# SBUF offsets of the matmul operands: stationary tiles at multiples of 64 bytes, moving weights 32 bytes off

## The chip, the cores and the metric

The kernel runs on one core of a Trainium2 chip. The metric is the device time of one launch in microseconds: the kernel before has a median of 1641.32 us over three runs (1641.16 to 1642.12). TensorE multiplies, VectorE (DVE), ScalarE (ACT) and GpSimd (POOL) do the rest, and the DMA queue of SyncE (SP) brings the weights in.

## The reference, cut to what matters

One transformer-like block on 256 tokens of width 2048, all in float32: a token mixer (spatial gating beside gated linear attention), a cross attention over a memory of 256 rows, and a feed-forward layer with a short convolution. Nearly all of its arithmetic is in products of an activation with a weight matrix:

```
z = h @ w_in                       # h 256x2048, w_in 2048x12304, cut into sg, q, k, v, og, ma, mb
merged = sigmoid(m_a) * (y_a @ w_proj_a) + sigmoid(m_b) * (y_b @ w_proj_b)
y = merged @ w_out
...                                # cross attention: xa_wq, xa_wk, xa_wv, xa_wo
hid = h @ w_up                     # 2048 x 11264
y = (gelu(gate) * up) @ w_down     # 5632 x 2048
```

## The kernel before, in words

**Split products.** A product in float32 is made of three in the type float32r: each operand x is split into `hi`, its rounding, and `lo` = x - `hi`, and the products hi*hi, hi*lo and lo*hi are summed in PSUM. A weight unit of 128 x 2048 comes in by one DMA (`load_raw`, three buffers `raw`), is split half by half by `split_half` (ACT rounds into `hi`, line 89; DVE subtracts into `lo`, line 90; four buffers of each, from the pool `wpool`), and is used at once. Activations are split once per stage by `split_psum`, and live in tiles of shape [128, k, 2, 256], hi beside lo: `hT`, `yaT`, `ybT`, `mT`, `fT`, `h2T` (also called `hT` in the code), `oT`, `act`.

**Two kinds of product.** A matmul has a stationary operand, brought into the array by a load (LDWEIGHTS, shown as PEld), and a moving one that streams past it.

- `tok_mm` (lines 106 to 108) is used in the stages sg, v, og, m, p, mix, xv, xa and ffn. The *activation* is stationary (128 columns), and 512 columns of `hi` or `lo` *weights* move. Three matmuls of 512 moving columns make one step.
- `feat_piece` (lines 137, 138, 140 and 141) is used in the stages k, q, xk, xq and up. The *weights* are stationary, and the activation moves: 512 columns against `hi` (its hi and lo halves together), 256 columns against `lo`. A pair of such matmuls makes one step. The stage up has 88 blocks of 16 pairs, k and q eight blocks each, xk and xq four each.

Line 449 writes out the first sg product, line 637 is the product `o` of the gated attention (moving `v`, stationary `AS`).

**What sets the order.** A scheduler orders the instructions from a model of times, except in the parts under `manual_schedule`. The pools place tiles one behind the other in SBUF, in the order in which they are opened, so a tile's address follows from the sizes of those before it. `const` and `stat` are small pools whose tiles begin at multiples of 32 bytes.

Of the kernel before, what the change touches and what calls it, by code (L numbers as in the profile page):

```python
# [11 lines left out]
F32 = mybir.dt.float32  # L12
F32R = mybir.dt.float32r
# [4 lines left out]
P = 128  # L18
# [3 lines left out]
KD = D // P  # L22
# [10 lines left out]
EPS = 1e-6  # L33
UW = 2048
HW = 1024

C_MIX, C_XA, C_MEM, C_FFN = 0, KD, 2 * KD, 3 * KD
C_CB = 4 * KD
# [6 lines left out]
def block_kernel(ctx: ExitStack, tc: tile.TileContext, a, out):  # L45
    nc = tc.nc

    def pool(stack, name, bufs=1, space=None, side=None):
        kw = {"space": space} if space is not None else {}
        if side is not None:  # L50
            kw["side"] = side
        return stack.enter_context(tc.tile_pool(name=name, bufs=bufs, **kw))

    const = pool(ctx, "const")
    wpool = pool(ctx, "wpool")
# [23 lines left out]
        while later:  # L79
            step()  # L80

    def split_half(raw, p=None, into=None, eng=None):
        p = wpool if p is None else p
        if into is None:
            hi = p.tile([P, HW], F32R, tag="hi", bufs=4, name="hi")
            lo = p.tile([P, HW], F32R, tag="lo", bufs=4, name="lo")
        else:
            hi, lo = into
        nc.scalar.copy(out=hi, in_=raw)  # L89
        (eng or nc.vector).tensor_tensor(out=lo, in0=raw, in1=hi.bitcast(F32), op=ALU.subtract)  # L90
        return hi, lo

    def load_raw(src):
        raw = wpool.tile([P, UW], F32, tag="raw", bufs=3, name="raw")
        nc.sync.dma_start(out=raw, in_=src)
        return [raw[:, i * HW:(i + 1) * HW] for i in range(UW // HW)]

    def pieces(w, n, nu):
        for u in range(nu):
            for half in load_raw(w[n, u]):  # L100
                yield split_half(half)

    def tok_mm(ps, xT, k, t, wh, wl, first, last):
        xh = xT[:, k, 0, t * P:(t + 1) * P]
# [5 lines left out]
    def tok_piece(ps, xT, i, t, hi, lo, K, nw=512):  # L110
        kp = HW // nw
        for kk in range(kp):
# [16 lines left out]

    def feat_piece(ps, xT, i, hi, lo, kks=range(HW // P)):  # L130
        for kk in kks:
# [10 lines left out]

    def feat_block(w, j, xT, name, srcs=None):
        ps = mm_psum(f"{name}_{j}")
        for i, (hi, lo) in enumerate(srcs if srcs is not None else pieces(w, j, KD * P // UW)):
            feat_piece(ps, xT, i, hi, lo)
            step()
        return ps
# [165 lines left out]
    mt = ctx.enter_context(ExitStack())  # L314
    with ExitStack() as mix:
        mp = pool(mix, "mp", side="left")
        hT = mp.tile([P, KD, NT, S], F32R, name="hT")
        yaT = mp.tile([P, SGW // P, NT, S], F32R, name="yaT")
        gl = mix.enter_context(ExitStack())
# [16 lines left out]
        with ExitStack() as st2:  # L336
# [67 lines left out]
            with tc.manual_schedule():  # L404
                nc.scalar.dma_start(out=gmix, in_=a["cols"][:, C_MIX:C_MIX + KD])
                first.append(wpool.tile([P, 2, 2, 512], F32, tag="raw", bufs=3, name="raw"))
                for k in (0, 1):
                    for n in range(2):
                        nc.sync.dma_start(out=first[0][:, n, k, :], in_=a["w_sgv"][0, :, n, k, :])
                        if n == 0:  # L410
                            load_xt(k, 1)
                load_xt(2, 2, nc.scalar)
                load_unit([(slice(0, 2), k) for k in range(2)])
                load_xt(4, 2)
                load_unit()
                warm_up(10)
                pss = [[mm_psum(f"sg_{n}_{t}") for t in range(NT)] for n in (2, 3)]
                for i in range(KD // 2):
                    if 1 <= i < KD // 2 - 2:
                        if i % 2:  # L420
                            load_xt(2 * i + 4, min(4, KD - 2 * i - 4))
                        load_unit()
                    hl = []
                    for n in range(2):
                        hi = wpool.tile([P, HW], F32R, tag="hi", bufs=4, name="hi")
                        lo = wpool.tile([P, HW], F32R, tag="lo", bufs=4, name="lo")
                        hl.append((hi, lo))
                    if i < 2:
                        for k in range(2):
                            c = slice(k * 512, (k + 1) * 512)  # L430
                            for n, (hi, lo) in enumerate(hl):
                                split_half(first[i][:, n, k, :], into=(hi[:, c], lo[:, c]))
                                if n == 0:
                                    gain_x(2 * i + k)
                    else:
                        gain_x(2 * i)
                        gain_x(2 * i + 1)
                        for n, x in enumerate(hl):
                            split_half(first[i][:, n, :, :].rearrange("p k c -> p (k c)"), into=x)
                    square_x(i)  # L440
                    later_loads(i)
                    for k in (2 * i, 2 * i + 1):
                        if k == KD - 1:
                            token_rstd()
                        c = slice(k % 2 * 512, (k % 2 + 1) * 512)
                        for n, (hi, lo) in enumerate(hl):
                            for j, (part, w) in enumerate(((0, hi), (1, hi), (0, lo))):
                                for t in range(NT):
                                    nc.tensor.matmul(pss[n][t], hT[:, k, part, t * P:(t + 1) * P], w[:, c],  # L449
                                                     start=k == 0 and j == 0, stop=k == KD - 1 and j == 2)  # L450
                ps = mm_psum("glr")
                for k in range(KD):
                    nc.tensor.matmul(ps[0:80, :], wg[:, k, :, :], hT[:, k, :, :], start=k == 0, stop=k == KD - 1)

                row_bcast(rs, rbc, "mix")
# [189 lines left out]

        mpool = pool(mt, "mtp", side="right")
        mT = mpool.tile([P, KD, NT, S], F32R, name="mT")
        with ExitStack() as st:
            sp = pool(st, "mg", side="right")
            for n in range(4):  # L650
                acc = [None] * NT
                for wm, wp, yT, K in ((a["w_ma"], a["w_pa"], yaT, SGW // P), (a["w_mb"], a["w_pb"], ybT, KD)):
                    ps = tok_block(wm, n, hT, KD, "m")
                    sgs = []
                    for t in range(NT):
                        sg = sp.tile([P, 512], F32, tag="sgm", bufs=3, name=f"sgm_{n}_{t}")
                        nc.scalar.activation(out=sg, in_=ps[t], func=AF.Sigmoid, scale=rs[t])
                        sgs.append(sg)
                    ps = tok_block(wp, n, yT, K, "p")
                    for t in range(NT):  # L660
                        pr = sp.tile([P, 512], F32, tag="pr", bufs=5, name=f"pr_{n}_{t}")
                        nc.vector.tensor_tensor(out=pr, in0=ps[t], in1=sgs[t], op=ALU.mult)
                        if acc[t] is None:
                            acc[t] = pr
                        else:
                            nc.vector.tensor_tensor(out=pr, in0=pr, in1=acc[t], op=ALU.add)
                            later.append(partial(transp_split, pr, t, mT, 4 * n, f"mt_{n}_{t}"))
            flush()
# [11 lines left out]
    with ExitStack() as xa:  # L680
# [106 lines left out]
        with tc.manual_schedule():  # L787
# [26 lines left out]
                        tok_piece(pss[n, t], oT, i, t, *early[2 * n + i], H)  # L814
            ups = [load_raw(a["w_up"][j, 0]) for j in (0, KF)]
            ups = [[raw[i] for raw in ups] for i in range(2)]
            ups[0] = [split_half(raw, eng=eng) for raw, eng in zip(ups[0], (nc.vector, nc.gpsimd))]
            for n in (0, 1):
                for t in range(NT):
                    pn.leave(pss[n, t], n, t, gain_first=t == 1)  # L820
# [52 lines left out]
            for q in range(4):  # L873
                gain_out2(tps[2 * q:2 * q + 2], C_FFN, fT, 2 * q)
                if q < 2:
                    pn.add(1, q + 2)
                    ups[1][q] = split_half(ups[1][q])
                if q == 3:
                    up1 = [split_half(half) for half in load_raw(a["w_up"][1, 0])]
                square3(1, q)  # L880
                for ps, (hi, lo) in zip(up_ps, ups[q // 2]):
                    feat_piece(ps, fT, q // 2, hi, lo, range(q % 2 * 4, q % 2 * 4 + 4))
                if q < 2:
                    up_in(q + 2)
# [7 lines left out]
    with ExitStack() as ff:  # L892
        fp = pool(ff, "ff", side="right")
        act = fp.tile([P, KF, NT, S], F32R, name="act")
        with ExitStack() as up:
            tp_ = pool(up, "tp_", side="left")
            rb3 = tp_.tile([P, S], F32, name="rb3")
# [128 lines left out]
```

## Time and profile before

| | us |
|---|---|
| median of three runs | 1641.32 |
| the profiled execution | 1642.16 |
| its span, first to last instruction | 1640.5 |
| TensorE busy with matmuls | 1628.3 |
| weight loads | 1372.4 |
| DVE busy | 1044.1 |
| ACT busy | 845.9 |

A matmul's busy time in the profile runs on past the start of the next one: matmuls are pipelined. Of use is the spacing from one start to the next. It is read either from rows of the timeline, or from a window full of matmuls, as its length over the number of matmuls in it. That number counts those that lie across the window's ends too. Where a matmul shows 0.39 us and the spacing is 0.227 us, some 1.7 are in flight at any time, and so many are counted too often.

### The profile page before, as it was taken

The page shows a single profiled execution, that of the slowest core. Times are in us where ns is not written, and L with a number is a line of the kernel's source. Part 1 is how long each engine was busy: PE and PEld are TensorE (multiplying, and loading weights), DVE is VectorE, ACT ScalarE, POOL GpSimd, SP SyncE. Part 2 cuts the span into 40 slices and gives each one's busy share as a digit, 9 for nine tenths or more (in the row PEclk, how much of TensorE's full clock was granted, in tenths as well). Part 3 has the DMA queues.
Part 4 walks back from the last instruction along what each step waited for, and adds up shares of the span by engine and source line. Part 5 has one row for each costly group of instructions (what it writes and reads, how often), then busy time and mean ns, then how long its engine had stood idle before and what let it go on. Part 6 is the DMA issues. An engine that isn't in the chain of part 4 may idle for free.

```text
span 1640.5 us, 20820 instructions
## 1 busy us (share of the span) xinstructions
PE 1628.3 (99%) x8090; PEld 1372.4 (84%) x8090; DVE 1044.1 (64%) x1398; ACT 845.9 (52%) x1174; POOL 40.0 (2%) x127
## 2 busy tenths in 40 slices
PE   9999999999999999999999999999999999999997
PEld 7888888888888888888888888888888888888886
DVE  7777645555454545465766877777777777444444
ACT  7764444444444444464656655555555555344342
POOL 0100000000000000000002000000000000000000
PEclk9999999999999999999999999999999999999999
DMA  9554455555555555595553555555545555555553
GB/s 330 180 196 168 172 200 179 178 178 180 186 192 191 190 195 183 204 356 196 189 206 103 189 191 186 182 184 199 181 180 191 191 183 206 205 181 198 187 199 107
DMA packets 47699, 315.43 MB, mean 192 GB/s; under 512 B 5392, under 2 KB 6032, under 8 KB 10864
## 3 DMA queue, kind: packets, MB, share of 16 engines
q1 hardware_dynamic: 47312, 313.83, 53.5%
q8 instruction: 63, 1.03, 0.2%
q14 instruction: 36, 0.29, 0.1%
q10 hardware_dynamic: 288, 0.27, 0.0%
HBM read 311.98 MB, written 2.10 MB: 191 GB/s over the span
## 4 chain that ended last, share of the span: by engine, by line
PE 96%; ACT 1%; DVE 1%; DMA 1%; issue 1%; SPq 0%; DVEq 0%; POOLq 0%; POOL 0%; ACTq 0%
PE up L137 19%; PE up L138 10%; PE ffn L106 5%; PE ffn L108 5%; PE ffn L107 5%; PE m L107 4%; PE m L106 4%; PE m L108 4%; PE p L107 3%; PE p L106 3%; PE p L108 3%; PE sg L449 2%; PE mix L108 2%; PE mix L107 2%; PE v L107 2%; PE v L108 2%
## 5 line engine op out<-in xcount | busy, mean ns | idle before, releaser
L90 DVE TENSOR_TENSOR lo<-raw,hi 128x1024 fp32r<-128x1024 f32 (+1 forms) x567 | 689.2, 1218 | 444.6 <-ACT hi L89 436.1
L89 ACT CAST hi<-raw 128x1024 fp32r<-128x1024 f32 (+1 forms) x568 | 591.5, 1044 | 524.5 <-PE ffn L107 129.6
L137 PE MATMUL up<-fT,hi 128*128 128x512 f32 x1320 | 470.4, 399 | 0.4 <-DVE fT L210 0.4
L138 PE MATMUL up<-fT,lo 128*128 128x256 f32 x1320 | 370.7, 281 | 0.0
L137 PEld LDWEIGHTS up<-fT,hi 128*128 128x128 f32 x1320 | 248.0, 188 | 57.6 <-DVE fT L210 0.7
L138 PEld LDWEIGHTS up<-fT,lo 128*128 128x128 f32 x1320 | 249.3, 189 | 4.2
L106 PE MATMUL ffn<-hi,act 128*128 128x512 f32 x352 | 138.7, 394 | 0.0
L108 PE MATMUL ffn<-lo,act 128*128 128x512 f32 x352 | 137.7, 392 | 0.0
L107 PE MATMUL ffn<-hi,act 128*128 128x512 f32 x352 | 136.6, 388 | 0.0
L903 ACT COPY hd<-up 128x256 f32<-128x256 f32 x88 | 32.8, 374 | 139.7 <-PE up L141 139.7
L106 PE MATMUL m<-hi,hT 128*128 128x512 f32 x256 | 100.0, 391 | 0.0
L108 PE MATMUL m<-lo,hT 128*128 128x512 f32 x256 | 99.9, 390 | 0.0
L107 PE MATMUL m<-hi,hT 128*128 128x512 f32 x256 | 99.7, 389 | 0.0
L904 DVE TENSOR_TENSOR hd<-up,hd 128x256 f32<-128x256 f32 x88 | 37.4, 425 | 74.8 <-ACT hd L903 74.8
L108 PEld LDWEIGHTS ffn<-lo,act 128*128 128x128 f32 x352 | 66.1, 188 | 15.5
L107 PEld LDWEIGHTS ffn<-hi,act 128*128 128x128 f32 x352 | 66.1, 188 | 14.8
L106 PEld LDWEIGHTS ffn<-hi,act 128*128 128x128 f32 x352 | 66.2, 188 | 13.1
L108 PEld LDWEIGHTS m<-lo,hT 128*128 128x128 f32 x256 | 48.0, 188 | 9.9
L106 PEld LDWEIGHTS m<-hi,hT 128*128 128x128 f32 x256 | 48.1, 188 | 9.9
L107 PEld LDWEIGHTS m<-hi,hT 128*128 128x128 f32 x256 | 48.1, 188 | 9.8
L907 ACT ACTIVATE cv<-hd,cols 128x256 f32<-128x256 f32 x88 | 52.7, 603 | 0.4
L106 PE MATMUL v<-hi,hT 128*128 128x512 f32 x128 | 50.5, 394 | 0.0
(303 smaller groups left out, 2469.5 us busy)
## 6 DMA issues: line engine op xcount, KB each, us to landing
raw<-in_w_up SPq DMA_DIRECT2D x88, 1024.0 KB, 4.8
raw<-in_w_dn SPq DMA_DIRECT2D x44, 1024.0 KB, 4.8
raw<-in_w_v SPq DMA_DIRECT2D x16, 1024.0 KB, 4.8
raw<-in_w_og SPq DMA_DIRECT2D x16, 1024.0 KB, 4.8
raw<-in_w_ma SPq DMA_DIRECT2D x16, 1024.0 KB, 4.8
raw<-in_w_mb SPq DMA_DIRECT2D x16, 1024.0 KB, 4.8
raw<-in_w_pb SPq DMA_DIRECT2D x16, 1024.0 KB, 4.8
raw<-in_w_o SPq DMA_DIRECT2D x16, 1024.0 KB, 4.9
```

The lines of the kernel that those rows point to most:

```text
L89: nc.scalar.copy(out=hi, in_=raw)
L90: (eng or nc.vector).tensor_tensor(out=lo, in0=raw, in1=hi.bitcast(F32), op=ALU.subtract)
L106: nc.tensor.matmul(ps, xh, wh, start=first, stop=False)
L107: nc.tensor.matmul(ps, xl, wh, start=False, stop=False)
L108: nc.tensor.matmul(ps, xh, wl, start=False, stop=last)
L137: nc.tensor.matmul(*big, start=k == 0, stop=False)
L138: nc.tensor.matmul(*small, start=False, stop=False)
L449: nc.tensor.matmul(pss[n][t], hT[:, k, part, t * P:(t + 1) * P], w[:, c], start=k == 0 and j == 0, stop=k == KD - 1 and j == 2)
L903: nc.scalar.copy(out=hd[:, 2:], in_=ps[:, S:2 * S])
L904: nc.vector.tensor_tensor(out=hd[:, 2:], in0=ps[:, 0:S], in1=hd[:, 2:], op=ALU.add)
L907: nc.scalar.activation(out=cv, in_=hd[:, 2:], func=AF.Identity, scale=cols[:, w0 + 2:w0 + 3], bias=cols[:, C_CB + j:C_CB + j + 1])
```

## The change

Only the addresses of tiles change. The four `hi` and four `lo` buffers become 16 columns (64 bytes) longer. A new helper `hi_lo` returns columns 0 to 1023 of such a buffer where the weights are to move, and columns 8 to 1031, so 32 bytes on, where they are to be stationary. Three pads of 8 columns (32 bytes) move `hT`, `yaT` and `ybT`, then `mT`, then `act` by 32 bytes. Every engine has the same instructions in the same order before and after, with the same waits; no row of the order differs but for buffer numbers and line numbers, so no rows of it are shown.

The addresses that the two built programs give the operands, modulo 128 bytes. Two values stand where the buffers of one name differ, since a buffer is now 4160 bytes long and was 4096:

| stage | matmuls | moving: before | after | stationary: before | after |
|---|---|---|---|---|---|
| up (`fT` moves, `hi`/`lo` stand) | 2816 | 32 | 32 | 32 | 0 or 64 |
| xk | 128 | 32 | 32 | 32 | 0 or 64 |
| xq | 128 | 96 | 96 | 32 | 0 or 64 |
| k, q (`hT` moves) | 512 | 32 | 64 | 32 | 0 or 64 |
| sg, v, og, m, p (`hi`/`lo` move) | 2496 | 32 | 32 or 96 | 32 | 64 |
| mix | 384 | 32 | 32 or 96 | 96 | 64 |
| ffn | 1056 | 32 | 32 or 96 | 96 | 64 |
| o (`v` moves, `AS` stands) | 36 | 96 | 96 | 32 | 64 |
| xv | 96 | 32 | 32 or 96 | 32 | 32 |
| xa, weights from their own pool | 48 | 96 | 32 or 96 | 96 | 96 |
| xa, weights held in `fT` | 48 | 32 | 32 | 96 | 96 |

The remaining matmuls are few, most of them in plain float32. Of these, `warm` has both operands at 64 modulo 128, before and after, and `att` both at 96.

```diff
+SH = 8
...
-    def split_half(raw, p=None, into=None, eng=None):
+    def hi_lo(p=None, c=0):
         p = wpool if p is None else p
+        return [p.tile([P, HW + 2 * SH], F32R, tag=n, bufs=4, name=n)[:, c:c + HW] for n in ("hi", "lo")]
+
+    def split_half(raw, p=None, into=None, eng=None, c=0):
         if into is None:
-            hi = p.tile([P, HW], F32R, tag="hi", bufs=4, name="hi")
-            lo = p.tile([P, HW], F32R, tag="lo", bufs=4, name="lo")
+            hi, lo = hi_lo(p, c)
...
-    def pieces(w, n, nu):
+    def pieces(w, n, nu, c=0):
         for u in range(nu):
             for half in load_raw(w[n, u]):
-                yield split_half(half)
+                yield split_half(half, c=c)
...
-        for i, (hi, lo) in enumerate(srcs if srcs is not None else pieces(w, j, KD * P // UW)):
+        for i, (hi, lo) in enumerate(srcs if srcs is not None else pieces(w, j, KD * P // UW, SH)):
...
         mp = pool(mix, "mp", side="left")
+        mp.tile([P, SH], F32, name="mp_pad")
         hT = mp.tile([P, KD, NT, S], F32R, name="hT")
...
         mT = mpool.tile([P, KD, NT, S], F32R, name="mT")
+        mpool.tile([P, SH], F32, name="mt_pad")
...
-                ups[1][q] = split_half(ups[1][q])
+                ups[1][q] = split_half(ups[1][q], c=SH)
...
         act = fp.tile([P, KF, NT, S], F32R, name="act")
+        fp.tile([P, SH], F32, name="act_pad")
```

## Rows read from the trace of the kernel before

**Rows 1.** The page: span, busy time by engine, and TensorE's granted clock (slices).
```profile
span 1640.5 us, 20820 instructions
...
PE 1628.3 (99%) x8090; PEld 1372.4 (84%) x8090; DVE 1044.1 (64%) x1398; ACT 845.9 (52%) x1174; POOL 40.0 (2%) x127
...
PEclk9999999999999999999999999999999999999999
```

**Rows 2.** Waits of PE, the longest two (us in total, times, longest us).
```profile
PE warm L174 <- POOL ones L64: 1.1, 1, 1.1
PE ntp_ffn L196 <- DVE x L275: 1.0, 1, 1.0
```

**Rows 3.** Windows of four stages: up, ffn, mix, and m with p.
```profile
core 0: us, PE busy (x) PEld busy (x) DVE busy (x) ACT busy (x) POOL busy (x), PEclk, DMA share, GB/s
912.00:1390.00 478.00, 478.00 (x2709) 414.65 (x2709) 379.37 (x601) 281.38 (x429) 8.53 (x85) 1.00 0.52 186
1391.00:1630.00 239.00, 239.00 (x1046) 196.11 (x1045) 110.98 (x103) 94.16 (x101) 0.27 (x1) 1.00 0.50 182
746.00:784.00 38.00, 38.00 (x168) 31.18 (x167) 18.57 (x20) 15.99 (x18) 0.00 (x0) 1.00 0.53 190
421.00:463.00 42.00, 42.00 (x187) 34.79 (x186) 19.41 (x17) 17.47 (x18) 0.00 (x0) 1.00 0.54 185
```

**Rows 4.** Timeline of PE in the stage up: start us, duration us, and the instruction.
```profile
1000.15 0.40 PE L137 MATMUL up<-fT,hi 128*128 128x512 f32 x1
1000.38 0.28 PE L138 MATMUL up<-fT,lo 128*128 128x256 f32 x1
1000.50 0.40 PE L137 MATMUL up<-fT,hi 128*128 128x512 f32 x1
...
1001.21 0.40 PE L137 MATMUL up<-fT,hi 128*128 128x512 f32 x1
```

**Rows 5.** Timeline of PE in the stage up, another place: three pairs.
```profile
922.84 0.39 PE L137 MATMUL up<-fT,hi 128*128 128x512 f32 x1
...
923.88 0.39 PE L137 MATMUL up<-fT,hi 128*128 128x512 f32 x1
```

**Rows 6.** Timeline of PE in the stage xa: weights of their own pool, then in fT.
```profile
871.26 0.39 PE L106 MATMUL xa<-hi,oT 128*128 128x512 f32 x1
...
873.98 0.39 PE L106 MATMUL xa<-hi,oT 128*128 128x512 f32 x1
...
876.05 0.39 PE L106 MATMUL xa<-fT,oT 128*128 128x512 f32 x1
...
878.80 0.39 PE L106 MATMUL xa<-fT,oT 128*128 128x512 f32 x1
```

**Rows 7.** Timeline of PE at the product o: nine matmuls in one row.
```profile
245.03 2.26 PE L637 MATMUL o<-v,AS 128*128 128x512 f32 x9
247.13 0.39 PE L106 MATMUL v<-hi,hT 128*128 128x512 f32 x1
```

**Rows 8.** Timeline of PE at a matmul that the next one follows late.
```profile
92.93 0.40 PE L106 MATMUL sg<-hi,hT 128*128 128x512 f32 x1
93.62 0.50 PE L108 MATMUL sg<-lo,hT 128*128 128x512 f32 x1 [0.29 <-DVE lo L90]
```

**Rows 9.** The same place, weight loads (PEld).
```profile
92.70 0.19 PEld L106 LDWEIGHTS sg<-hi,hT 128*128 128x128 f32 x1
93.62 0.19 PEld L108 LDWEIGHTS sg<-lo,hT 128*128 128x128 f32 x1 [0.73 <-DVE lo L90]
```

**Rows 10.** Float32 matmuls and their loads by tile: ns min/median/max, first and last start.
```profile
L174 PE MATMUL warm<-ones x10: 275/275/275, 886.5 to 889.9; 128*128 128x128 f32 x10
L174 PEld LDWEIGHTS warm<-ones x10: 190/192/192, 886.4 to 889.8; 128*128 128x128 f32 x10
L580 PE MATMUL att<-QT,KT x48: 270/275/275, 131.4 to 208.6; 128*128 128x128 f32 x48
L580 PEld LDWEIGHTS att<-QT,KT x48: 187/192/192, 131.3 to 208.5; 128*128 128x128 f32 x48
```

More of the change, by code (lines that the diff above doesn't have):

```diff
@@ L424, in block_kernel @@
                     for n in range(2):
-                        hi = wpool.tile([P, HW], F32R, tag="hi", bufs=4, name="hi")
-                        lo = wpool.tile([P, HW], F32R, tag="lo", bufs=4, name="lo")
-                        hl.append((hi, lo))
+                        hl.append(hi_lo())
                     if i < 2:
@@ L816, in block_kernel @@
             ups = [[raw[i] for raw in ups] for i in range(2)]
-            ups[0] = [split_half(raw, eng=eng) for raw, eng in zip(ups[0], (nc.vector, nc.gpsimd))]
+            ups[0] = [split_half(raw, eng=eng, c=SH) for raw, eng in zip(ups[0], (nc.vector, nc.gpsimd))]
             for n in (0, 1):
@@ L876, in block_kernel @@
                     pn.add(1, q + 2)
-                    ups[1][q] = split_half(ups[1][q])
+                    ups[1][q] = split_half(ups[1][q], c=SH)
                 if q == 3:
-                    up1 = [split_half(half) for half in load_raw(a["w_up"][1, 0])]
+                    up1 = [split_half(half, c=SH) for half in load_raw(a["w_up"][1, 0])]
                 square3(1, q)
```

## The prediction

> **What bounds the kernel now.** The page comes first: PE is busy for 1628.3 of 1640.5 us, its clock is granted in full in every slice (the 2.4 GHz level), and DVE and ACT have 36% and 48% of the span to spare [rows 1]. Then PE's waits: the longest are 1.1 and 1.0 us [rows 2]. So the kernel is one stream of about 8,000 matmuls, and a change that leaves every instruction in its place can only alter how fast that stream runs.
>
> How fast it runs is read from the spacing of starts. In m and p, 42 us hold 187 - 1.7 matmuls of 512 columns: 226.7 ns each. In ffn it is 239 / (1046 - 1.7) = 228.9 ns, in mix 38 / (168 - 1.7) = 228.5 ns. In up, 478 us hold some 2,707 matmuls, half with 512 and half with 256 columns: 353.2 ns a pair [rows 3]. In detail, three pairs of up take 1.06 us, 353.3 ns each [rows 4].
>
> **Does the place of an operand bear on it?** Three readings say yes, one says no.
>
> In xa, one stage with one stationary tile, twelve matmuls take 873.98 - 871.26 = 2.72 us, 226.7 ns each, with moving weights at 96 (modulo 128), and 878.80 - 876.05 = 2.75 us, 229.2 ns each, with moving weights at 32 [rows 6]. The stationary tile is at 96 in both. Stages m and p, where both operands are at 32, give 226.7; ffn and mix, with 32 and 96, give 228.9 and 228.5 [rows 3]. The product o, with the moving operand at 96 and the stationary one at 32, takes 2.10 us for nine, 233.3 ns each [rows 7]. So the distance between the two operands, modulo 128, has a price: none at distance 0, 2 to 7 ns at distance 64.
>
> At one and the same set of addresses, up has a second pace: near 923 us three pairs take 1.04 us, 346.7 ns each, not 353.3 [rows 5]. The paces lie 6.67 ns apart, and so do 226.7 and 233.3. That is 16 cycles at the granted 2.4 GHz. 226.7 ns is 34 such steps, for 512 columns of 4 bytes, or 32 times 64 bytes of each partition; 353.3 ns is 53 steps, for 48 times 64 bytes. I read a step as the reading of 64 bytes (an estimate from these rows), and the steps over 32 and over 48 as lost: two of a matmul of 512 columns, five of a pair. Over 4,000 of the one and 1,792 of the other that is 13.3 x 4000 + 33.3 x 1792 = 113 us, all the room there is. What loses them may be two streams, weights and moving data, in each other's way, locked into a pattern that depends on where each starts.
>
> Against it stands the matmul at 92.93 us. The next weight load comes 0.69 us later, so nothing is loaded beside it [rows 9], and yet it shows 0.40 us [rows 8], no less than the 0.39 of those with a load beside them. By that row the 13.3 ns belong to the moving stream alone, and the stationary tile can't touch them. Nor does a load by itself take longer at an odd half of 64 bytes: 192 ns with a stationary tile at 64 (warm) and 192 ns at 96 (att) [rows 10].
>
> **The change, part by part.** The pads and the longer buffers cost no instruction. The splits on ACT and DVE write to other offsets; they stay in the cover of 36% and 48% idle time, in up 21% and 41% (379.4 and 281.4 of 478 us) [rows 3]. I put them at nothing. If DVE's splits grew by more than a quarter in up, DVE would be the bound there; no row shows such a growth, nor excludes it.
>
> What is left is that the stationary operand goes to a multiple of 64 while the moving one stays 32 bytes off it. No fp32r row shows this distance (32 or 96, modulo 128): the trace has 0 and 64 alone. So the cost is bounded by the nearest rows.
>
> - Lowest: no step lost, 213.3 and 106.7 ns by the count of steps above; that is the 113 us.
> - Highest: each matmul one step of 6.67 ns later, as in o [rows 7].
> - What I take: every matmul goes to the lowest steady pace that the rows show for its size, because the steps above that pace are those that vary with the place, and the pace itself is the one that the lone matmul shows. For 512 columns this is 226.7 ns. For 256 columns I take half of it, 113.3 ns, which is just under the 0.12 us between starts at 1000.38 and 1000.50 [rows 4]. A pair then takes 340.0 ns.
>
> The sum, against the profiled execution:
>
> - Pairs with shifted weights and an unshifted activation: up 88 x 16 = 1408, xk 64, xq 64, together 1536. 1536 x (353.3 - 340.0) = 20.4 us.
> - ffn: 1056 x (228.9 - 226.7) = 2.3 us. mix: 384 x (228.5 - 226.7) = 0.7 us. o: 36 x 6.6 = 0.2 us.
> - sg, v, og, m, p (2496 matmuls) run at 226.7 already: nothing.
> - k and q, 256 pairs: here the activation moves too, to 64, so the distance is again 0 or 64, and I leave them as they are. xv and xa keep their stationary tiles: nothing.
>
> Together 23.6 us. 1642.16 - 23.6 = 1618.6; the profiled execution lies 0.84 above the median, so **1617.7 us**, 1.4% faster. Where the stall goes, nothing is late next: raw halves are split ahead of PE, and PE's waits stay small unless it runs faster by more than DVE's spare fifth in up.
>
> **The rivals.**
>
> *The pace itself falls.* If the two steps over 32 are the two streams' doing too, one step more goes: 3972 matmuls of 512 columns with a shifted stationary tile (sg, v, og, m, p, mix, ffn, o) and the 1536 of up, xk and xq, each 6.67 ns: 36.7 us beyond the forecast, 1581 us. Two steps would give some 1544. For it: what is lost comes in whole steps, like the part that varies with the place. Against it: the lone matmul of [rows 8].
>
> *A new collision.* Distance 32 is half of 64, and distance 64 costs. If 32 puts a step onto every matmul, as the 233.3 ns of o [rows 7], then 2496 x 6.67 = 16.6 us in sg to p, 1440 x 4.5 = 6.5 us in ffn and mix, and 1536 x 6.67 = 10.2 us in the pairs: 33 us, **1674 us**. It decides against the change as soon as the spacing in m and p is over 229 ns without a gain in up. For it: the pattern in which m and p have locked, at distance 0, is the best that the trace has, and the change gives it up for 2496 matmuls. Against it: the pairs of up are locked at their worse pace now, and hold the most time.
>
> *Nothing moves.* If the paces depend on the place by whole 64 bytes alone, or on the moving stream alone, the time stays at 1641 us. Then the distance within 64 bytes plays no part, and ffn and mix may change by their 3 us at most. For it: the lone matmul, and loads of 192 ns at either offset [rows 10]. The Trainium skill, "SBUF — State Buffer", section "Who interferes with whom", has it so: TensorE reads the moving operand and the weights through two ports of their own, and "PE and ACT never wait on anyone". By that rule the change is worth nothing and the sum is 1641 us; by the rows it is not, since the 226.7 and 229.2 ns of [rows 6] differ by the moving operand's place alone. The trace so agrees with the rule for the lone matmul, and not for xa.
>
> **How the numbers follow.** Chances: the forecast 0.32, with a range of its own from 1600 to 1636; the falling pace (under 1600) 0.28; nothing 0.14; a new collision 0.26. So faster by over 0.2% is 0.60, within 0.2% (1638 to 1645, about what a measurement of this kernel can tell from no change) 0.14, slower 0.26. The forecast is the likeliest, hence 1617.7. The range takes in the forecast's own, one step of the falling pace and a part of its second, no change, and the cheaper half of the collision: 1562 to 1660. About 0.1 is left out at either end.
>
> **What would show it.** In the changed kernel's windows: three pairs of up in 1.02 us would be the forecast (340.0 a pair), 1.06 no change, under 1.00 the falling pace, over 1.07 the collision. In m and p 226.7 is the forecast, 220 the falling pace, 233 the collision. ffn and mix should come to the spacing of m and p. k and q tell whether an aligned pair of operands is better or worse than one with 32 bytes between. The forecast is wrong if m and p change their spacing at all, for then the pace isn't the moving stream's own; it is wrong also if up stays at 353 ns.

## The result: 1657.67 us, 1% slower

The changed kernel has a median of 1657.67 us (1657.54 to 1658.1, four runs) against 1641.3 us for the kernel before, a ratio of 1.0099 (95% interval 1.0083 to 1.0115). The forecast of 1617.7 us had the wrong sign. The time lies inside the range and above the bound for "slower".

The page of the changed kernel, to be read against [rows 1], and its longest waits of PE (us in total, times, longest us), against [rows 2]:

```profile
span 1656.4 us, 20820 instructions
...
PE 1645.0 (99%) x8090; PEld 1372.8 (83%) x8090; DVE 1043.1 (63%) x1398; ACT 844.9 (51%) x1174; POOL 38.7 (2%) x127
...
PEclk9999999999999999999999999999999999999999
```

```profile
PE warm L177 <- POOL ones L65: 1.1, 1, 1.1
PE ntp_ffn L199 <- DVE x L278: 1.0, 1, 1.0
```

PE's busy time grew by 16.7 us and the span by 15.9. Nothing else moved: the clock is granted in full, DVE and ACT are within 1.0 us of before, weight loads within 0.4, and the waits are the same two. So the cover that the prediction counted on held, and the matmuls themselves run slower.

Windows of up, ffn and m with p (columns as in [rows 3]):

```profile
925.50:1397.50 472.00, 472.00 (x2707) 413.86 (x2706) 376.21 (x599) 280.42 (x428) 8.52 (x85) 1.00 0.53 190
1406.00:1645.00 239.00, 239.00 (x1025) 192.28 (x1024) 106.71 (x96) 91.48 (x97) 0.00 (x0) 1.00 0.49 176
426.00:468.00 42.00, 42.00 (x182) 33.80 (x181) 19.76 (x18) 16.88 (x17) 0.00 (x0) 1.00 0.55 197
```

With the same correction as for [rows 3], up has a pair of matmuls every 472 / 2705 x 2 = 349.0 ns (before 353.2), ffn a matmul every 239 / (1025 - 1.7) = 233.6 ns (before 228.9), m and p every 42 / (182 - 1.7) = 232.9 ns (before 226.7). Of these stages up gained, and the others lost.

The timeline of PE in up shows two paces side by side, as [rows 4] and [rows 5] did: five pairs in 1.77 us (354 ns each), and, a few microseconds on, five in 1.73 us (346).

```profile
1100.29 0.40 PE L140 MATMUL up<-fT,hi 128*128 128x512 f32 x1
...
1102.06 0.39 PE L140 MATMUL up<-fT,hi 128*128 128x512 f32 x1
...
1105.57 0.39 PE L140 MATMUL up<-fT,hi 128*128 128x512 f32 x1
...
1107.30 0.39 PE L140 MATMUL up<-fT,hi 128*128 128x512 f32 x1
```

Summed by stage, as spacings from the start of each matmul to the start of the next, over the whole trace:

| stage | before, us | after, us | difference |
|---|---|---|---|
| up, 512 columns | 332.8 | 326.0 | -6.8 |
| up, 256 columns | 165.6 | 166.8 | +1.2 |
| ffn | 241.5 | 246.4 | +4.9 |
| m | 175.0 | 179.9 | +4.9 |
| p | 130.6 | 134.4 | +3.9 |
| og | 87.0 | 89.6 | +2.6 |
| v | 88.1 | 90.4 | +2.3 |
| mix | 88.2 | 89.9 | +1.7 |
| sg | 89.3 | 90.5 | +1.2 |
| k, q, xk, xq, xv, xa, o together | | | +0.1 |

The differences are taken before rounding. They make +15.9 us, all that the span grew by. The question for the experiments was what sets the pace of a matmul, since neither a wait nor another engine is in play.

### The profile page after: what moved, and what is told of

It is laid out like the page before. It is cut to its first block, busy times and chain, and to the rows that moved or that the text cites. A ratio compares the mean times of both kernels' runs of the same rounds, so it can differ in the third digit from the quotient of the medians.

```text
span 1656.4 us, 20820 instructions
## 1 busy us (share of the span) xinstructions
PE 1645.0 (99%) x8090; PEld 1372.8 (83%) x8090; DVE 1043.1 (63%) x1398; ACT 844.9 (51%) x1174; POOL 38.7 (2%) x127
## 4 chain that ended last, share of the span: by engine, by line
PE 98%; DMA 1%; issue 0%; ACT 0%; DVE 0%; SPq 0%; DVEq 0%; POOLq 0%; POOL 0%; ACTq 0%
PE up L140 18%; PE up L141 9%; PE ffn L111 5%; PE ffn L109 5%; PE ffn L110 5%; PE m L111 4%; PE m L110 4%; PE m L109 4%; PE p L109 3%; PE p L110 3%; PE p L111 3%; PE sg L451 2%; PE v L111 2%; PE og L109 2%; PE v L110 2%; PE mix L109 2%
```

## The experiments

The theory at the start was that of the prediction, amended by the result: the pace follows the distance between moving and stationary operand; distance 32 is good for pairs and bad for the `tok_mm` stages. The rivals were that it is the place of one operand by itself, or the length of the buffers. In what follows, the distance is the address of the moving operand less that of the stationary one. Stages with `tok_mm` are called tok stages.

### Only the weights of the pair stages are shifted

```diff
+PAD = 32
...
+    def hi_lo(p=None, c=0):
+        n = HW + (PAD if p is wpool else 0)
+        c = c if p is wpool else 0
+        return [p.tile([P, n], F32R, tag=t, bufs=4, name=t)[:, c:c + HW] for t in ("hi", "lo")]
...
-        for i, (hi, lo) in enumerate(srcs if srcs is not None else pieces(w, j, KD * P // UW)):
+        for i, (hi, lo) in enumerate(srcs if srcs is not None else pieces(w, j, KD * P // UW, 24)):
```

The stationary weights of up, k, q, xk and xq go 96 bytes on, to 0 modulo 128. The `hi` and `lo` buffers become 128 bytes longer, so that in the tok stages every operand stays where it was, modulo 128.

> Only the weights that stand (k, q, xk, xq, up) are shifted, all of them to 0 modulo 128; the buffers are 128 bytes longer, so that every buffer has the same place. The product stages sg to p, mix and ffn keep their places. Theory 'distance' (the pace of a stage is set by the distance of moving and stationary operand, modulo 128): a pair of up at 346.7 ns as in the half of the changed kernel's blocks that stood at 0, 1408 x 6.6 = 9 us, with k, q and xk some 11 us less: 1630 us; m and p stay at 226.7 ns. Rival 'taking turns' (what moved in the changed kernel came from buffers whose places alternate between two values, so that no pattern can lock): up stays at 353 ns, 1641 us.

Measured: 1642.72 us, a ratio of 1.0009 (0.9999 to 1.0018): no difference. Windows of up and of m with p:

```profile
912.00:1384.00 472.00, 472.00 (x2725) 416.44 (x2724) 378.85 (x604) 281.51 (x430) 9.85 (x87) 1.00 0.53 192
421.00:463.00 42.00, 42.00 (x184) 34.19 (x184) 20.29 (x18) 16.87 (x17) 0.00 (x0) 1.00 0.54 197
```

Up came to 472 / 2723 x 2 = 346.7 ns a pair, 8.8 us less over the stage. But m and p, with not one address changed modulo 128, went to 42 / (184 - 1.7) = 230.4 ns. Unit by unit the trace shows why: their matmuls now run at 226.7 ns (behind three of 230 to 233 at a unit's start) and at 232.7 ns, in turn with the buffer. Buffers that are 128 bytes longer stand alternately at distance 0 and 128 *modulo 256*. So the period isn't 128 bytes, as the prediction's table of addresses has it, and the table's "32 or 96" hides four distances: 32, 96, 160 and 224.

### Only the three pads

```diff
+        mp.tile([P, 8], F32, name="mp_pad")
...
+        mpool.tile([P, 8], F32, name="mt_pad")
...
+        fp.tile([P, 8], F32, name="act_pad")
```

The activations move by 32 bytes, the weights stay.

> Only the three pads of 32 bytes, so hT, yaT, ybT, mT and act stand at 64; hi and lo stay as before, all at 32. The distance in sg, v, og, m, p, mix and ffn is the same for every matmul. Distance: these stages lose as much as in the changed kernel, 233 to 234 ns per matmul, 21 us in all: 1662 us, with up unchanged at 353 ns. Taking turns: with one place for all buffers the stream locks again, 226.7 to 229 ns: 1639 to 1645 us.

Measured: 1661.76 us, a ratio of 1.0125 (1.0109 to 1.014). Windows of up, ffn and m with p:

```profile
925.50:1397.50 472.00, 472.00 (x2676) 409.51 (x2675) 373.16 (x591) 277.93 (x424) 8.51 (x85) 1.00 0.52 187
1409.00:1648.00 239.00, 239.00 (x1026) 192.24 (x1025) 108.88 (x99) 92.08 (x97) 0.00 (x0) 1.00 0.50 179
426.00:468.00 42.00, 42.00 (x182) 33.82 (x181) 19.76 (x18) 16.94 (x17) 0.00 (x0) 1.00 0.54 197
```

Up keeps its 353 ns (472 / 2674 x 2), and the tok stages lose all that the change loses: ffn 233.3 ns, m and p 232.9. In the units of m, p and og the distance is now constantly 224, and every matmul takes 233.3 ns. So the loss needs no alternation of buffers, and it comes with the pads alone. Their loss less up's gain, 20.4 - 5.6 = 14.8 us, is most of the change's 16.4.

### Everything moved together by 32 bytes

```diff
+    const.tile([P, 8], F32, name="c_pad")
...
+        mpool.tile([P, 24], F32, name="mt_pad")
...
+        fp.tile([P, 24], F32, name="act_pad")
```

A pad in the first pool moves all that is placed behind it. `mT` and `act` are moved once more, by 96 bytes, so that their distance to the weights keeps its value modulo 128 (64), but not modulo 256 (192 where it was 64).

> Everything is moved together: both operands go to 64 in up, k, q, sg, v, og, m and p (distance 0, as before), and to 64 and 0 in mix and ffn (distance 64, as before). Distance: nothing changes in any of these stages, 1640 to 1643 us. Rival 'place' (an operand at an odd half of 64 bytes costs by itself, whatever the other does): 226.7 ns in m and p and 353 ns in up fall, by at least one step of 6.67 ns each, 1600 us or less.

Measured: 1647.34 us, a ratio of 1.0035 (1.0021 to 1.005). Windows of up, ffn and m with p:

```profile
908.00:1386.00 478.00, 478.00 (x2710) 414.72 (x2709) 377.84 (x597) 279.89 (x429) 8.45 (x85) 1.00 0.52 187
1394.00:1633.00 239.00, 239.00 (x1026) 191.58 (x1025) 107.87 (x97) 91.53 (x97) 0.00 (x0) 1.00 0.49 178
420.00:462.00 42.00, 42.00 (x187) 34.78 (x186) 19.41 (x17) 17.56 (x18) 0.00 (x0) 1.00 0.52 185
```

Where both operands moved by the same 32 bytes, nothing changed: m and p 226.7 ns, up 353. So the place of an operand by itself has no price here. ffn went from 228.9 to 233.3 ns (+4.7 us) and mix lost 1.7 us, with the distance the same modulo 128 and another modulo 256. That is the second reading against a period of 128.

### A sweep of the distance by 16 bytes

```diff
+        for i, (hi, lo) in enumerate(srcs if srcs is not None else pieces(w, j, KD * P // UW, 4 * (j % KF % 8) if name == "up" else 0)):
...
+        nu = K * 512 // UW
+        turn = (lambda n, u: 4 * ((n * nu + u) * 8 // (4 * nu))) if keep else 0
```

In up the offset of the weights in their buffer goes round by block, in ffn by unit; the buffers are 128 bytes longer as above.

> A map in one run: in up the stationary weights of the blocks take eight places in turn, 16 bytes apart (distance 32, 16, 0, ... modulo 128), in ffn the moving weights take eight places, five or six units of weights at each. Distance: the pace depends on the place in a regular manner, 353 ns at distance 0 and 347 ns at 32 in up, 226.7 ns at 0, 229 at 64 and 233 at 32 and 96 in ffn; places that are odd multiples of 16 bytes fall between. Place: the pace in up differs between multiples of 32 and odd multiples of 16, and not among the former.

One run gave 1649.44 us. In the table are mean spacings of the units at each distance modulo 256, in ns. Where the changed kernel or the runs above hold one of these distances in m, p, og, ffn or up, they agree within 1.5 ns, save up at distance 0, where the pairs have two paces, 346 and 353 ns, as [rows 4, 5] showed:

| distance | tok, 512 columns | pair of up | distance | tok, 512 columns | pair of up |
|---|---|---|---|---|---|
| 0 | 227.0 | 350.4 | 128 | 232.9 | 350.2 |
| 16 | 231.6 | 346.4 | 144 | 233.4 | 353.1 |
| 32 | 233.3 | 346.7 | 160 | 234.3 | 346.9 |
| 48 | 233.4 | 350.0 | 176 | 231.2 | 352.8 |
| 64 | 229.0 | 353.2 | 192 | 233.2 | 353.0 |
| 80 | 231.2 | 349.9 | 208 | 234.6 | 347.3 |
| 96 | 233.6 | 349.8 | 224 | 233.3 | 352.2 |
| 112 | 231.1 | 349.0 | 240 | 233.2 | 346.9 |

The changed kernel's stages are sums of this table: its tok stages sit at 32, 96, 160 and 224 in turn (233.3, 233.6, 234.3, 233.3: mean 233.6, as its window of ffn shows), its up at the same four (346.7, 349.8, 346.9, 352.2: mean 348.9, its window shows 349.0). For tok, all four are among the worse places; for pairs, two of four are good.

Some entries are means of two paces. Up at 0 has 346.5 to 348.4 ns in its first blocks and 353.3 in the later ones, up at 224 has 346.7 in its first and 353.3 in the other five, and tok at 240 has one unit at 226.7 and two at 236.7. From the first two of these units:

```profile
1489.02 0.39 PE L112 MATMUL ffn<-hi,act 128*128 128x512 f32 x1
...
1493.78 0.39 PE L112 MATMUL ffn<-hi,act 128*128 128x512 f32 x1
...
1500.93 0.40 PE L113 MATMUL ffn<-lo,act 128*128 128x512 f32 x1
...
1505.19 0.40 PE L113 MATMUL ffn<-lo,act 128*128 128x512 f32 x1
```

Twenty-one spacings in 4.76 us are 226.7 ns each, eighteen in 4.26 us are 236.7. Both units use the same weight buffers, and the distance is 240 throughout. What differs is the place of the activation's columns, 16,384 bytes further on in the second unit, and the unit before: its distance was 96 for the first, and 112 for the second and the third. So the distance doesn't always fix the pace alone. What ran before seems to have a say, and no run tests how.

### The distances chosen from the sweep

```diff
+        mpool.tile([P, 48], F32, name="mt_pad")
...
+    ftp.tile([P, 8], F32, name="ft_pad")
...
+        hp.tile([P, 40], F32, name="h2_pad")
...
+        fp.tile([P, 48], F32, name="act_pad")
```

Pads alone, with the buffers at their old length: distance 32 in up, xk and xq, and 0 in mix and ffn; sg, v, og, m and p keep their 0.

> Made from the kernel before with four pads and no change of the weight buffers: fT goes up by 32 bytes (distance 32 in up and xk), mT and act down by 192 (distance 0, modulo 256, in mix and ffn), h2T down by 160 (distance 32 in xq). Theory 'distance modulo 256' (the pace of a stage is a function of the moving operand's address less the stationary one's, modulo 256; in the four runs so far 0 is the best for 512-column steps, 226.7 ns, and 32 or 160 for pairs, 346.7 ns): up 1408 x 6.6 = 9.3 us less, xk and xq 0.7 less, ffn 1056 x 2.2 = 2.3 less, mix 0.8 less, xv 96 x 6.6 = 0.6 more since fT also stands there: 1641.3 - 12.5 = 1629 us. Rival 'history' (a stage locks into a pattern that depends on what ran before and on the buffers' turns, and a place is good only by chance): each stage may go either way, within 6 us of 1641.

Measured: 1631.42 us against 1641.67 for the kernel before, a ratio of 0.9937 (0.9924 to 0.9951). It is faster than both kernels. The first line of its page, and windows of up, ffn and m with p:

```profile
span 1629.6 us, 20820 instructions
...
905.00:1377.00 472.00, 472.00 (x2717) 416.18 (x2716) 377.99 (x600) 281.10 (x429) 8.71 (x86) 1.00 0.53 191
1384.00:1618.00 234.00, 234.00 (x1034) 193.74 (x1033) 108.95 (x99) 92.74 (x98) 0.00 (x0) 1.00 0.51 183
421.00:463.00 42.00, 42.00 (x187) 34.78 (x186) 19.55 (x16) 16.99 (x17) 0.00 (x0) 1.00 0.53 185
```

Up is at 472 / 2715 x 2 = 347.7 ns a pair (-7.4 us over the stage), ffn at 234 / (1034 - 1.7) = 226.7 (-2.3), mix 0.8 us less, and m and p still at 226.7. So at these distances the sweep's table holds as a recipe, not as a description only. The rival by which a place is good only by chance, from what ran before, doesn't account for this run; at other distances, such as 240 above, history has a part.

### A finer sweep, by 4 bytes

```diff
+PAD = 64
...
+        for i, (hi, lo) in enumerate(srcs if srcs is not None else pieces(w, j, KD * P // UW, j % KF if name == "up" else 0)):
...
+        turn = (lambda n, u: n * nu + u) if keep else 0
```

The offset grows by one column with each block of up and each unit of ffn. The buffers are 256 bytes longer, so that the distances of all other stages keep their value modulo 256. A few work tiles get one buffer less to make room, and a pad moves `act` so that ffn starts at distance 0.

> A finer map: the place of the stationary weights in up rises by 4 bytes from one block pair to the next (43 places, distances 252 down to 84, modulo 256), that of the moving weights in ffn by 4 bytes from one unit to the next (44 places, distances 0 to 172). The buffers are 256 bytes longer, so all four have the same place modulo 256. Distance modulo 256: the paces of the places that are known come again (ffn 226.7 ns at 0, 231.6 at 16, 233.3 at 32, 229.0 at 64; up 346.7 at 240 and 160, 353 at 224, 192, 176 and 144), with steps or slopes of at most 7 ns between them. If only the 64-byte stretch in which an operand begins counts, the pace is constant within 64 bytes. History: the known paces don't come again. In both theories the stages sg, v, og, m and p run at 226.7 ns throughout, since buffers longer by 256 bytes keep their distance at 0.

One run gave 1642.72 us. Two units of ffn, at distance 20 and at distance 28:

```profile
1415.39 0.40 PE L111 MATMUL ffn<-hi,act 128*128 128x512 f32 x1
...
1420.19 0.40 PE L113 MATMUL ffn<-lo,act 128*128 128x512 f32 x1
...
1426.04 0.39 PE L111 MATMUL ffn<-hi,act 128*128 128x512 f32 x1
...
1431.03 0.39 PE L112 MATMUL ffn<-hi,act 128*128 128x512 f32 x1
```

Twenty spacings in 4.80 us, 240.0 ns each, and, 8 bytes on, twenty-two in 4.99 us, 226.8 ns each. From 0 on in steps of 4 bytes, ffn shows 226.6, 236.7, 233.4, 228.9, 231.7, 240.0, 233.2, 226.6 and, at 32, 233.3 ns. So the pace depends on single columns of 4 bytes, not on blocks of 16, 32 or 64 bytes, and I found no rule that gives the values. Two things are regular. In ffn the multiples of 16 repeat the coarse sweep within 0.5 ns. And nothing falls under 226.6 ns in ffn or 346 ns a pair in up, as means of a unit or a block. In up, six distances (100, 136, 148, 156, 180 and 236) have two paces, 3 to 7 ns apart, in their two blocks: at 180, one block runs at 353.3 and the other at 346.7 ns. The tok stages that kept their distance modulo 256 also kept 226.7 ns (m, p and og within 0.1 us of the kernel before), which bears out the period of 256.

### Shorter weight loads

```diff
+    def part_mm(ps, xT, k, t, wh, wl, K, m):
+        for j, (part, wt) in enumerate(((0, wh), (1, wh), (0, wl))):
+            first, last = k == 0 and j == 0, k == K - 1 and j == 2
+            cols = P if first or last else m
+            nc.tensor.matmul(ps[0:cols, :], xT[:, k, part, t * P:t * P + cols], wt, start=first, stop=last)
```

What remains is the 13.3 ns between the best 226.7 ns and the 213.3 ns that the prediction counted as the floor (32 steps of 6.67 ns, an estimate; no run shows it). If loads and moving data share something, a shorter load should give part of it back. In three of og's four heads the matmuls load 64, 32 or 96 columns and stream the same 512. The kernel leaves out what the missing columns would add to the result.

> In the stage og alone most matmuls load fewer stationary columns: head 0 keeps 128, head 1 has 64, head 2 has 32, head 3 has 96 (all but the first and the last matmul of each product; the other output rows lack these terms). The moving columns stay 512, the places too. Theory 'two streams' (what a matmul takes over 213 ns is lost to the weight load that runs beside it): the 13.3 ns shrink with the load, to 220 ns per matmul with 64 columns, 217 with 32, 223 with 96. Rival 'own stream' (the moving stream loses two steps whatever is loaded): 226.7 ns for every head.

The loads got shorter, and the matmuls did not get faster. The loads by shape (ns, least, median and largest), and PE in the head with 64 columns and in the one with 32:

```profile
L121 PEld LDWEIGHTS og<-hi,hT x192: 107/134/188, 269.0 to 384.6; 128*64 128x64 f32 x62, 128*32 128x32 f32 x62, 128*96 128x96 f32 x62, 128*128 128x128 f32 x6
```

```profile
273.80 0.39 PE L121 MATMUL og<-lo,hT 128*64 128x512 f32 x1
...
285.52 0.40 PE L121 MATMUL og<-lo,hT 128*64 128x512 f32 x1
...
334.17 0.62 PE L121 MATMUL og<-hi,hT 128*32 128x512 f32 x2
...
336.26 0.63 PE L121 MATMUL og<-hi,hT 128*32 128x512 f32 x2
```

The shortest load, with 32 columns, takes 107 ns where one of 128 takes 188, and the one with 64 takes 134. PE needs 11.72 us for 51 spacings, 229.8 ns each, with 64 columns; 2.09 us for 9, 232 ns each, with 32; and the head with 96 shows 230.2; all more than 226.7 with 128. So what is lost isn't in proportion to what is loaded. That a shorter load makes the pace worse at one and the same distance suggests that the load takes part in the variable share, through its timing and not through its amount; a shorter load also writes fewer rows of output, and the two weren't separated. The fixed share is left where the lone matmul of [rows 8] put it, with the moving stream.

### Operands of two bytes

```diff
+    def short_pieces(w, n, nu, p, c):
+        for u in range(nu):
+            for raw in load_raw(w[n, u]):
+                hi, lo = [p.tile([P, HW + 32], BF16, tag=t, bufs=2, name=t)[:, c:c + HW] for t in ("bhi", "blo")]
+                nc.scalar.copy(out=hi, in_=raw)
+                nc.vector.tensor_tensor(out=lo, in0=raw, in1=hi, op=ALU.subtract)
+                yield hi, lo
...
-                ogps = tok_block(a["w_og"], h, hT, KD, "og")
+                if h == 0:
+                    ogps = tok_block(a["w_og"], h, hT, KD, "og")
+                else:
+                    ogps = tok_block(a["w_og"], h, h16, KD, "og",
+                                     srcs=short_pieces(a["w_og"], h, KD * 512 // UW, hp16, (0, 0, 16, 32)[h]))
```

> Heads 1 to 3 of the stage og take operands of two bytes (the activation and both halves of the weights in bf16, so that part is computed less exactly); head 0 stays in float32r, and all else is as before. Each matmul still streams 512 columns against 128 loaded ones. The distances of the two-byte operands differ by head: 0, 64, 128, 192 in head 1; 32, 96, 160, 224 in head 2; 0, 64, 128, 192 in head 3. Theory A: the 13.3 ns over 512 cycles, and what varies with the distance, come from fetching 4 bytes a column. With half the bytes each of the three heads comes under 220 ns, whatever its distance. Theory B: they come from the hand-over between one matmul and the next, whatever the width: heads 1 and 3 give 226.7 to 233 ns, and head 2 again some 233 ns, as its distances do in float32r.

One run gave 1639.52 us. PE in heads 1 and 3 of og, and a load in head 1:

```profile
269.62 0.38 PE L116 MATMUL og<-bhi,h 128*128 128x512 bf16 x1
...
273.50 0.38 PE L116 MATMUL og<-bhi,h 128*128 128x512 bf16 x1
...
361.15 0.38 PE L116 MATMUL og<-bhi,h 128*128 128x512 bf16 x1
...
365.90 0.38 PE L117 MATMUL og<-blo,h 128*128 128x512 bf16 x1
```

```profile
269.62 0.10 PEld L117 LDWEIGHTS <-h 128*128 128x128 bf16 x1
```

18 spacings in 3.88 us, 215.6 ns each, and 22 in 4.75 us, 215.9 ns each. In all three heads the spacings of two-byte matmuls are 215 or 216 ns (the first behind a float32r one and the last before one aside), at the distances 0, 32, 64, 96, 128, 160, 192 and 224 alike; head 0, in float32r, kept 226.7. So 11 of the 13.3 ns go away with the width of the operands, and the dependence on distance goes altogether. The hand-over theory falls. The Trainium skill, "TensorE: Matmul & The Clock Gate", section "Wait — 56ns, not 53.3ns?", gives 215.7 ns for 512 columns once warm; the two-byte rows here agree, and the four-byte rows lie 11 to 24 ns above it.

The kernel makes both operands narrower at once, their type changes with the width, and a load then takes 0.10 us and not 0.19. Which of these matters most wasn't separated; the shorter four-byte loads of the run before speak for the moving one.

## Why the prediction failed, point by point

**What bounds the kernel: right.** One stream of matmuls, paced by nothing but itself. The splits at other offsets cost nothing, as DVE's and ACT's busy times show, and no wait appeared.

**That distance has a price: right.** The readings of [rows 3] and [rows 6] were of this effect: distance 0 gives 226.7 ns, distance 64 gives 229, at other places too, and moving both operands together changes nothing.

**Modulo 128: wrong.** I reduced the addresses to 128 bytes because the trace's distances, 0 and 64, looked like half a period. The period is 256 bytes. The prediction's rows held a warning: o, at 64 modulo 128, took 233.3 ns [rows 7], and ffn, at 64 modulo 128, took 228.9 [rows 3]. Two paces at one distance were a sign that the variable was not the right one. (Modulo 256 o stands at 192 and ffn at 64, where the sweep has 233.2 and 229.0 ns.) I used the 233.3 as an upper bound and went on.

**The step that failed: "every matmul goes to the lowest steady pace that the rows show for its size".** This took the best pace as the norm and each worse one as a disturbance that an unseen distance would remove. The opposite holds. 226.7 ns is reached at few distances (0, 28, 60 and 156 of the 44 places that the fine sweep visited in ffn), and 31 of the 44 give over 231. A distance drawn blind should have been put near the common pace, not at the best.

The terms, with what they measured:

| term | forecast, us | measured, us |
|---|---|---|
| up, xk, xq (1536 pairs) | -20.4 | -5.9 |
| sg, v, og, m, p | 0 | +14.8 |
| ffn and mix | -3.0 | +6.6 |
| o, k, q, xv, xa | -0.2 | +0.4 |
| sum | -23.6 | +15.9 |

- *Pairs.* Sign right, size 3.4 times too large, for two reasons. The pace of 340.0 ns was made by halving 226.7 for the 256-column matmul; no run shows it. The best block has 346 ns a pair, and as 512-column matmuls in up got faster (236.4 to 231.5 ns), the 256-column ones got slower (117.6 to 118.4). And only two of the four distances that a longer buffer gives are good ones.
- *sg to p: "run at 226.7 already: nothing".* This is the term that turned the sign. They stood at one of the few best distances modulo 256 and were moved off it. It was written as a stage with nothing to gain, and should have been read as one with everything to lose.
- *ffn and mix.* They were taken to go down to 226.7 ns and went up to 233.6.

**The rivals.** *A new collision* had the mechanism and the price of the tok stages: 16.6 and 6.5 us against 14.8 and 6.6 measured. Its condition, over 229 ns in m and p "without a gain in up", was half met, since up gained 5.6 us where the rival asked for a loss of 10.2 in the pairs. That tie of the pairs to the tok stages was the error of all three cases: I let one distance act alike on both kinds of matmul. The sweep shows them nearly unrelated (distance 32: bad for tok, good for pairs; 64: good for tok, 353.2 ns and so among the worst for pairs). *The pace itself falls* is excluded for every distance tried: no tok unit went under 226.6 ns. *Nothing moves* falls too, and with it what the prediction drew from the rule of the Trainium skill ("SBUF — State Buffer", section "Who interferes with whom"): by that rule the spacing could not depend on where the other operand lies, and in ffn it runs from 226.6 to 240.0 ns as the weights move by 4 bytes a unit. Whether the two ports as such are independent no run here tests.

**The lone matmul** [rows 8] was read rightly as far as it goes. In a stream a matmul's duration lies 161 to 164 ns above its spacing (389 ns at 226.7, 404 at 240.0), so 0.40 us with nothing loaded beside it is no faster pace, and no placing of the operands went below 226.6 ns. That the base pace is the moving stream's own fits this and the shorter loads, and is argued: no run narrows the moving operand alone. The pace as a whole isn't, by the prediction's own sign: m and p did change their spacing, from 226.7 to 232.9 ns.

## What to carry to other kernels

When a kernel is one unbroken stream of float32r matmuls, the relative addresses of moving and stationary operands are worth some 1% (here 1.0% lost by the change, 0.6% gained by chosen pads): read the spacing of starts stage by stage, sweep the distance in one run by rotating an offset through the blocks, and choose by the table. A stage that already shows the lowest pace is at risk from any change of layout, a longer buffer included, and belongs in the sum as a possible loss. If one distance shows two paces, suspect the modulus first; a second pace can remain at the right one, as at 240, so a chosen place has to be measured.

## What the hardware showed that was not expected

- The spacing of float32r matmuls depends on the distance of their operands modulo 256 bytes, down to single columns of 4 bytes: 226.6 to 240.0 ns for 512 columns, 346 to 363 ns for a pair of 512 and 256, in which the weights stand and the activation moves. Moving both together by 32 bytes had no effect.
- At some distances there are two steady paces: 226.7 and 236.7 ns in ffn at 240, 346.7 and 353.3 ns a pair in up at 180.
- With two-byte operands the same matmul takes 215.6 to 215.9 ns at every distance tried.
- A shorter load (134 or 107 ns in place of 188) at an unchanged distance made the spacing worse, 229.8 and 232 in place of 226.7 ns.

Open remain why certain distances are good, what decides between two paces at one distance, what fixes the 226.6 ns, and whether the width of the moving operand alone would do what that of both did. That two four-byte streams lock into a pattern of accesses is consistent with all runs, and is argued, not shown.
